# One decoder layer on one core: w_out split two units ahead, norms and token sums in pieces, first feed-forward matrix by column halves

## The chip, the cores and the metric

The kernel runs on one core of a Trainium2 chip. The metric is device time in microseconds (us) for the whole program, the median of several executions. Engines are named as in the profile: PE (matmuls), DVE and ACT (element work), POOL (element work on SBUF), SP (issues the loads and stores). L12 is line 12 of the kernel.

## What is computed

One layer of a hybrid decoder for 1024 tokens of width 1024, in float32. Every matmul is made of three: each operand is split into a high and a low part, and high*high, high*low and low*high are summed.

```python
h = rmsnorm(x, norm_mix_g)
u, q, kc, vc, ks, vs, kw, vw, g_nsa, g_br = split(h @ w_in)
y_a = s5_mixer(u, ...) @ w_up_ssm                  # state-space scan, GLU
kc, vc = gelu(blocks(kc) @ w1_k) @ w2_k, ...       # compress(): 63 blocks of 32 tokens
y_b = nsa_mixer(q, kc, vc, ks, vs, kw, vw, gates, rel_bias) @ w_up_nsa
g_a, g_b = split(sigmoid(g_br))
x = x + (g_a * y_a + g_b * y_b) @ w_out            # "merge"
h = rmsnorm(x, norm_ffn_g)
x = x + (silu(h @ w_ffn_gate) * (h @ w_ffn_up)) @ w_ffn_down
return rmsnorm(x, norm_final_g)
```

## The kernel before

There is no scheduler: each engine works through its instructions in the order in which the code issues them, and waits at the head of its queue. What waits there holds everything behind it.

**Input projection and S5.** `in_proj` is a generator whose steps are three matmuls of 128x512 each. `along(s5_params, 4.0)` and `along(s5, 3.0)` let that many projection steps follow each yield of the S5 code; afterwards `beside(proj, rest, 0.459)` lets 0.459 yields of `compress` and `glu` follow each projection step. The projection is thus the filling between dependent S5 and compress steps.

**compress.** `keys(0)` loads the tokens of the keys as `kk` (four DMAs of 252 KB), DVE adds positions into `kv` (L990), and PE multiplies with the `w1` pieces (L1004, 16 matmuls each). `kk` has one buffer, so `keys(1)` waits for the first add.

**Attention.** `up(a)` is a generator; its last parts store `pad` to DRAM (L1087) and its buffers are needed by the softmax transposes (`ready()`). `start(2)` issues the 12 loads of V.

**Weights.** `W.next(...)` hands out a unit of a weight matrix in high and low parts (`wh` by ACT, L396; `wl` by DVE, L399). It first splits up to the unit after the one handed out and loads up to four ahead. There are two raw buffers and three of `wh`/`wl`.

**Merge and first.** `merge` multiplies with `w_out` in 20 units of 256 rows and 512 columns (q is the half of the columns): two passes over token tiles (0,1,4,5), q=0 and q=1, one over (2,3,6,7) for q=0, then (2,3) and (6,7) apart for q=1. A tile's part of a unit is six matmuls (L1442 to L1444). After the last unit of a pass DVE adds x to each bank (`add`, L1448), and for q=1 ACT squares (L1452), takes the root (L413), and scales (`norm`, L1456). The normed tile is transposed by PE. For tiles 4 to 7 `turn` makes the token-side Winograd operands in five pieces, T1, B22, T3, T2 and T4, each split on ACT and DVE; their tiles are T1h/T1l (piece T3), T0h/T0l (piece T2) and T2h/T2l (piece T4). The feed-forward matrices are then multiplied by seven products each (`product(n, i)`, 12 matmuls; L227 to L229). `first` is the first matrix, n=0, during which tiles 6 and 7 are still being turned; `rest(n)` the others. On the weight side POOL scales by the norm's gain (`scale`, L171) and makes `sums` S (L204 to L207), and `t1` to `t4` split the parts for the products: (1,2), (6,5), (7,3), (4).

**down.** 44 units; `sr` is the hidden activation read back from DRAM. `after()` is run at three points inside the last `rest` and starts the loads and splits of down.

Of the kernel before, what the change touches and what calls it, by code (L numbers as in the profile page):

```python
# [8 lines left out]
F32 = mybir.dt.float32  # L9
# [7 lines left out]
P = 128  # L17
# [116 lines left out]
class Winograd:  # L134
# [87 lines left out]
    def product(self, n, i, ps, first=True):  # L222

        (wh, wl), (bh, bl) = self.w.pop((n, i)), self.B[i]
        mm = self.K.nc.tensor.matmul
        for k in range(4):
            mm(ps, wh[:, k], bh[:, k], start=first and k == 0, stop=False, skip_group_check=True)  # L227
            mm(ps, wh[:, k], bl[:, k], start=False, stop=False, skip_group_check=True)  # L228
            mm(ps, wl[:, k], bh[:, k], start=False, stop=k == 3, skip_group_check=True)  # L229
# [5 lines left out]
    def p1(self, n):  # L235
        K = self.K
        x = self.x[n] = K.bank("a")
        self.product(n, 1, x)
        p = self.p[n] = self.tile("p1")
        K.nc.scalar.copy(p, x)  # L240
# [11 lines left out]
    def p2(self, n):  # L252
        K, (name, j) = self.K, self.mats[n]
        x = self.x.pop(n)
        self.product(n, 2, x, first=False)
        t = self.tile("x11")
        if name == "w_ffn_gate":
            K.nc.scalar.activation(t, x, AF.Silu)
            self.gates[j, 0, 0] = t
        else:  # L260
            K.nc.vector.tensor_tensor(t, x, self.gates.pop((j, 0, 0)), op=OP.mult)
            K.nc.sync.dma_start(self.sd[2 * j][0], t)

    def first(self, turn):


        V, GP = self.K.nc.vector, self.K.nc.gpsimd
        self.p1(0)
        self.t2(0)
        self.p1(1)  # L270
        turn("transpose", 6)
        turn("T1", 6)
        self.p2(0)
        turn("transpose", 7)
        turn("T1", 7)
        self.t3(0)
        self.p2(1)
        z5, z3, v, y, c = (self.K.bank(t) for t in "aabbc")
        self.product(0, 5, z5)
        turn("B22", 6)  # L280
        turn("B22", 7)
        self.t4(0)
        self.load(2)
        self.product(0, 3, z3)
        turn("T3", 6)
        turn("T3", 7)
        self.product(0, 7, v)
        turn("T2", 6)
        turn("T2", 7)
        self.product(0, 6, y)  # L290
        turn("T4", 6)
        turn("T4", 7)
        u2, p5, u3 = self.p.pop(0), self.tile("p1"), self.tile("x11")
        self.K.nc.scalar.copy(p5, z5)
# [12 lines left out]

    def rest(self, n, early):

        K, last = self.K, n + 1 == len(self.mats)  # L310
        V, AC, GP = K.nc.vector, K.nc.scalar, K.nc.gpsimd
        y = K.bank("b")
        self.product(n, 6, y)
        u2 = self.p.pop(n)
        V.tensor_tensor(u2, u2, y, op=OP.add)
        if not early:
            self.p2(n)
            self.t4(n)
# [20 lines left out]
        if last:  # L339
            next(self.after)  # L340
# [19 lines left out]
class Kernel:  # L360
# [589 lines left out]
    def compress(self, pool):  # L950
# [9 lines left out]
        def keys(which):  # L960
            kk = pool.tile([P, 2, 1008], F32, name="kk", tag="kk", bufs=1)
            for g in range(2):
                src = self.cd[which, 64 * g:64 * g + 64, :]
                nc.sync.dma_start(kk[0:64, g, :], src[:, 0:1008])
                nc.sync.dma_start(kk[64:128, g, :], src[:, 16:1024])
            return kk

        kk = keys(0)
        src = [A["cmp_w1_" + kind].rearrange("(e l d) h -> e d l h", e=2, l=16) for kind in "kv"]

        def w1(j):
            w = pool.tile([P, 4, 256], F32, name="w1", tag="w1", bufs=4)
# [15 lines left out]
        for which in range(2):  # L988
            kv = pool.tile([P, 16, 126], F32, name="kv", tag="kv", bufs=2)
            V.tensor_tensor(kv, kk.rearrange("p g (n l) -> p l (g n)", l=16),  # L990
                            pt[:, which, :, None].to_broadcast([P, 16, 126]), op=OP.add)
            kvs.append(kv)
            if which == 0:
                kk = keys(1)
            yield
            yield
        hids = []
        for which in range(2):
            t = self.bank("c")
            for j in range(4):  # L1000
# [6 lines left out]
                if which == 0:  # L1007
                    ws.append(w1(j + 4))
# [160 lines left out]
    def attention(self, pools, loads, up):  # L1169
# [254 lines left out]
    def merge(self, pool, m, td, xd, ffn):  # L1424
# [21 lines left out]
        def add(tt, q, o):  # L1446
            x = x1[tt][:, 512 * q:512 * q + 512]
            V.tensor_tensor(x, x, o, op=OP.add)  # L1448
            if q:
                sq[tt] = pool.tile([P, 1], F32, name="ss", tag="ss", bufs=4)  # L1450
                xns[tt] = pool.tile([P, D], F32, name="xn", tag="xn", bufs=4)
                AC.activation(xns[tt], x1[tt], AF.Square, accum_out=sq[tt])  # L1452
                nc.sync.dma_start(xd[tt], x1[tt])

        def norm(tt):
            AC.activation(xns[tt], x1.pop(tt), AF.Copy, scale=self.rstd(pool, sq.pop(tt)))  # L1456

        def turn(what, tt):
# [3 lines left out]
            if what == "transpose":  # L1462
                xs, ps[tt] = xns.pop(tt), [self.bank(t) for t in "bc"]
# [5 lines left out]
            if what == "T1":  # L1469
# [6 lines left out]
                V.tensor_tensor(t3, b22, pb, op=OP.subtract)  # L1476
                x, o = t1, [x[:, 0:4, at] for x in m]
            else:
                b22, t1, t3 = tmp[tt]
            if what == "B22":  # L1480
# [12 lines left out]
        def turned(tt):  # L1493
            if tt < 4:
                self.transposed("bc", xns.pop(tt), m[0], m[1], tt)
            else:
                for what in ("transpose", "T1", "B22", "T3", "T2", "T4"):
                    turn(what, tt)

        def units(tts, q, between):  # L1500
            banks = [self.bank("a") for _ in tts]
            for u in range(4):
                w = unit(u, q)
                for f, *a in between.get((u, "w"), ()):
                    f(*a)
# [9 lines left out]
        units((0, 1, 4, 5), 0, {(0, "w"): [(load, tt) for tt in (0, 1, 4, 5)] + [(ffn.factors,)]})  # L1515
        units((0, 1, 4, 5), 1, {3: [(norm, 5)]})
        units((2, 3, 6, 7), 0, {0: [(turned, 0)], 1: [(turned, 1), (turned, 4)],
                                (1, "w"): [(load, 2), (load, 3)], (2, "w"): [(load, 6), (load, 7)],
                                2: [(turned, 5)], (3, "w"): [(ffn.load, 0)], 3: [(ffn.sums, 0)]})
        units((2, 3), 1, {3: [(norm, 3)]})  # L1520
        units((6, 7), 1, {1: [(turned, 2)], (2, "w"): [(ffn.load, 1)], 2: [(turned, 3), (ffn.t1, 0)],
                          (3, "w"): [(ffn.scale, 1), (ffn.t1, 1)], 3: [(norm, 7)]})
        ffn.first(turn)


# [20 lines left out]
    def down(self, pool, loads, xd):  # L1546

        nc, V, AC, mm = self.nc, self.nc.vector, self.nc.scalar, self.nc.tensor.matmul
        gf = self.broadcast_row(pool, "gfin", self.A["norm_final_g"])
# [19 lines left out]
        for n, (h, f) in enumerate(order):  # L1569
# [5 lines left out]
            wh, wl = self.W.next("w_ffn_down", P * f, 1, 0, D, ("act", "dve"))  # L1575
            if f == 16:
# [33 lines left out]
    def program(self):  # L1610
# [60 lines left out]
        beside(proj, side, 0.459)  # L1671
# [59 lines left out]
        def after():  # L1731
            loads[2](2)
# [3 lines left out]
            W.ahead(1, 2)  # L1736
            loads[3](1)
            yield
# [83 lines left out]
```

## Time and profile before

| | |
|---|---|
| runs | 1663.34, 1660.53, 1663.0 us; median 1663.0 |
| profiled execution | 1657.91 us, its span 1656.0 us |
| PE clock granted, mean | 0.974 of full speed |
| PE, DVE, ACT, POOL busy | 1568.5, 923.9, 628.2, 644.1 us |

Idle time of PE is what to look for, and stretches with the clock below 1. A time of a stretch is to be read against that stretch's own rows.

### The profile page before, as it was taken

To read this page: it belongs to the slowest core of one execution; us is meant where nothing else is said; L and a number is where in the kernel's file an instruction comes from. 1 tells how busy PE (TensorE), PEld (TensorE's weight loads), DVE (VectorE), ACT (ScalarE), POOL (GpSimd) and SP (SyncE) were. 2 spreads that over 40 slices of the span, in tenths; PEclk is the share of its full clock that TensorE was granted. 3 is DMA by queue.
4 is the path that set the end of the run, shared out by engine and by line. 5 is a ranking of instruction groups with operands and counts; after the bars stand their busy time and mean duration, and the time that the engine had idled before them with its cause. 6 is when DMAs were issued, how large, how long until landed. Compare 5 with 4: busy or idle time off the path is not lost.

```text
span 1656.0 us, 22273 instructions
## 1 busy us (share of the span) xinstructions
PE 1568.5 (95%) x7868; PEld 1312.0 (79%) x7868; DVE 923.9 (56%) x1738; ACT 628.2 (38%) x1272; POOL 644.1 (39%) x742
## 2 busy tenths in 40 slices
PE   8998999998998899998997889999999998999995
PEld 7776788887887799998886668888888886888884
DVE  7365787712335799998945565444444443334433
ACT  5221234312211698997014443233233332223422
POOL 1007767500121455554500328666776661000001
PEclk9999999999999999999998889999999999999998
DMA  7343343376338712102553422222322214454551
GB/s 216 103 131 98 100 137 92 92 166 160 120 114 226 202 34 60 42 27 61 194 165 128 153 70 77 89 84 82 95 78 89 77 52 159 152 184 157 181 188 60
DMA packets 164582, 194.27 MB, mean 117 GB/s; under 512 B 20730, under 2 KB 119446, under 8 KB 164471
## 3 DMA queue, kind: packets, MB, share of 16 engines
q1 hardware_dynamic: 164471, 192.85, 37.9%
q8 instruction: 63, 1.03, 0.3%
q14 instruction: 48, 0.39, 0.1%
HBM read 142.87 MB, written 47.84 MB: 115 GB/s over the span
## 4 chain that ended last, share of the span: by engine, by line
PE 75%; DVE 8%; DMA 6%; ACT 4%; issue 3%; POOL 1%; SPq 1%; POOLq 0%; DVEq 0%; ACTq 0%
PE a L387 6%; PE a L388 6%; PE a L389 6%; PE a L227 4%; PE a L228 4%; PE a L229 4%; PE O L1305 3%; PE S L1189 3%; PE T L1287 3%; PE a L1585 2%; PE a L1586 2%; PE a L1584 2%; PE b L229 2%; PE b L228 2%; PE b L227 2%
## 5 line engine op out<-in xcount | busy, mean ns | idle before, releaser
L399 DVE TENSOR_TENSOR wl<-wr,wh 128x1024 fp32r<-128x1024 f32 (+1 forms) x166 | 193.9, 1180 | 133.6 <-ACT wh L396 113.1
L387 PE MATMUL a<-hhi,wh 128*128 128x512 f32 x448 | 183.5, 410 | 0.0
L389 PE MATMUL a<-hhi,wl 128*128 128x512 f32 x448 | 178.6, 399 | 0.0
L388 PE MATMUL a<-hlo,wh 128*128 128x512 f32 x448 | 178.2, 398 | 0.0
L1260 POOL TENSOR_SCALAR P<-P,sum,gates 128x640 f32<-128x640 f32 (+3 forms) x192 | 124.7, 663 | 125.0 <-DVE sum L1254 65.5
L396 ACT CAST wh<-wr 128x1024 fp32r<-128x1024 f32 (+1 forms) x134 | 109.7, 837 | 163.6 <-DMA wr<-in_w_out 53.6
L228 PE MATMUL a<-mlo,wh 128*128 128x512 f32 x352 | 138.4, 393 | 1.9 <-DVE mlo L399 1.9
L227 PE MATMUL a<-mhi,wh 128*128 128x512 f32 x352 | 138.8, 394 | 0.5 <-ACT p L240 0.5
L229 PE MATMUL a<-mhi,wl 128*128 128x512 f32 x352 | 138.5, 394 | 0.0
L171 POOL TENSOR_SCALAR wr<-wr,gcol 128x256 f32<-128x256 f32 x176 | 92.6, 545 | 91.2 <-DMA wr<-in_w_ffn_gate 76.5
L394 POOL TENSOR_SCALAR wh<-wr 128x1024 fp32r<-128x1024 f32 x32 | 35.1, 1099 | 226.8 <-PE a L388 158.7
L1289 DVE TENSOR_TENSOR PTl<-T,PTh 128x512 fp32r<-128x512 f32 (+3 forms) x200 | 104.2, 544 | 15.5 <-ACT PTh L1288 14.0
L387 PEld LDWEIGHTS a<-hhi,wh 128*128 128x128 f32 x448 | 85.6, 191 | 23.9 <-issue 6.2
L389 PEld LDWEIGHTS a<-hhi,wl 128*128 128x128 f32 x448 | 85.3, 190 | 20.1
L399 DVE TENSOR_TENSOR slo<-sr,shi 128x512 fp32r<-128x512 f32 x44 | 31.5, 717 | 124.7 <-ACT shi L396 124.7
L388 PEld LDWEIGHTS a<-hlo,wh 128*128 128x128 f32 x448 | 85.6, 191 | 17.8
L1240 ACT ACTIVATE P<-P,m 128x640 f32<-128x640 f32 (+7 forms) x128 | 95.7, 747 | 9.5 <-DVE m L1224 9.5
L441 POOL TENSOR_SCALAR x1f<-x1f,rstd 128x1024 f32<-128x1024 f32 (+1 forms) x2 | 2.3, 1150 | 247.7 <-DVE rstd L421 242.7
L1288 ACT CAST PTh<-T 128x512 fp32r<-128x512 f32 (+3 forms) x200 | 88.5, 475 | 26.5 <-PE T L1287 19.4
L1287 PE MATMUL T<-cst,P 128*128 128x128 f32 x592 | 88.2, 276 | 8.3 <-DVE PTl L1289 7.8
L1224 DVE CUSTOM_DVE_ANT_0 P<-S,B 128x640 f32<-128x640 f32 (+7 forms) x128 | 89.5, 700 | 5.2 <-PE S L1189 3.0
L396 ACT CAST shi<-sr 128x512 fp32r<-128x512 f32 x44 | 27.3, 619 | 164.2 <-PE c L1585 149.0
(421 smaller groups left out, 4050.1 us busy)
## 6 DMA issues: line engine op xcount, KB each, us to landing
wr<-in_w_ffn_down SPq DMA_DIRECT2D x44, 512.0 KB, 3.4
wr<-in_w_in SPq DMA_DIRECT2D x28, 512.0 KB, 4.3
wr<-in_w_ffn_gate SPq DMA_DIRECT2D x22, 512.0 KB, 3.8
wr<-in_w_ffn_up SPq DMA_DIRECT2D x22, 512.0 KB, 4.1
sr<-sd SPq DMA_DIRECT2D x44, 256.0 KB, 3.6
wr<-in_w_out SPq DMA_DIRECT2D x20, 512.0 KB, 4.3
gd<-evf SPq DMA_DIRECT2D x32, 256.0 KB, 2.4
Q<-qd SPq DMA_DIRECT2D x64, 128.0 KB, 3.2
```

Source lines behind the costliest of these rows:

```text
L227: mm(ps, wh[:, k], bh[:, k], start=first and k == 0, stop=False, skip_group_check=True)
L228: mm(ps, wh[:, k], bl[:, k], start=False, stop=False, skip_group_check=True)
L229: mm(ps, wl[:, k], bh[:, k], start=False, stop=k == 3, skip_group_check=True)
L387: mm(ps, a, c, start=start and k == 0, stop=False, skip_group_check=True)
L388: mm(ps, a, d, start=False, stop=False, skip_group_check=True)
L389: mm(ps, b, c, start=False, stop=stop and k == nk - 1, skip_group_check=True)
L396: nc.scalar.copy(hi, src)
L399: (nc.gpsimd if lo_eng == "pool" else nc.vector).tensor_tensor(lo, src, hi, op=OP.subtract)
L1240: AC.activation(p[:, 0:nk], p[:, 0:nk], AF.Exp, bias=m[:, 0:1], scale=-1.0, accum_out=sm(0))
L1260: sc = lambda x, y, z: GP.tensor_scalar(x, x, a[:, y:y + 1], gate(z), op0=OP.mult, op1=OP.mult)
L1287: T.transpose(t[:, x, :], p[:, c:c + P], self.ident)
L1289: V.tensor_tensor(ol, t[:, 0:len(cc), :], oh, op=OP.subtract)
```

## The change

It reorders; it computes the same, with 60 more PE instructions (five products are made in two halves of 256 columns).

1. The paces 4.0, 3.0 and 0.459 become 4.6, 3.2 and 0.6.
2. compress loads both `kk` up front (two buffers), ahead of `w1` (three buffers instead of four).
3. The remaining parts of `up(a)` run at the start of `start(2)`, ahead of the V loads.
4. In merge the split of unit u+2 is issued after the first tile of unit u (`W.ahead(2, 4)`). `square`, `root` and `norm` are separate and placed by hand; the pieces of `turn` for tiles 4 and 5 are spread over the units. In `first` both p1 products come up front, norms of tiles 6 and 7 are interleaved, and products 5, 6, 3, 7 and 4 are made by column halves: half 0 (tiles 4, 5) early, half 1 (tiles 6, 7) late.
5. down: four `sr` loads early, `gfin` later, and the third step of `after()` ahead of a store.

```diff
-    def first(self, turn):
+    def first(self, norms, turn):
...
-        self.p1(0)
+        x0, x1 = self.x[0], self.x[1] = bank("a"), bank("a")
+        self.product(0, 1, x0)
+        self.product(1, 1, x1)
+        next(norms)
         self.t2(0)
-        self.p1(1)
-        turn("transpose", 6)
+        next(norms)
+        self.p1out(0)
+        z5 = bank("a")
+        self.product(0, 5, z5, half=0)
+        turn("transpose", 6, "bc")
+        next(norms)
+        self.p1out(1)
+        turn("sums", 6)
+        y = bank("b")
+        self.product(0, 6, y, half=0)
...
+        self.product(0, 6, y, half=1)
+        self.sums(1)
+        AC.copy(p5, z5)
+        self.t2(1)
         V.tensor_tensor(u2, u2, y, op=OP.add)
         V.tensor_tensor(u3, u2, v, op=OP.add)
         V.tensor_tensor(u2, u2, z3, op=OP.add)
-        self.sums(1)
-        self.t2(1)
-        self.product(0, 4, c)
         GP.tensor_tensor(u2, u2, p5, op=OP.add)
         GP.tensor_tensor(p5, u3, p5, op=OP.add)
+        self.product(0, 4, c, half=1)
...
+        if last:
+            next(self.after)
         self.out(n, 1, 1, p5)
...
-            kk = pool.tile([P, 2, 1008], F32, name="kk", tag="kk", bufs=1)
+            kk = pool.tile([P, 2, 1008], F32, name="kk", tag="kk", bufs=2)
...
-        kk = keys(0)
+        ks = [keys(0), keys(1)]
...
-        ws = [w1(j) for j in range(4)]
+        ws = [w1(j) for j in range(3)]
...
             if n == 2:
+                run(up)
                 load_v(0, 5, 3)
...
                 for i, tt in enumerate(tts):
                     part(w, u, tt, banks[i])
+                    if i == 0:
+                        self.W.ahead(2, 4)
+                        for f, *a in between.get((u, "m"), ()):
+                            f(*a)
                     if u == 3:
                         add(tt, q, banks[i])
-                        if q and i:
-                            norm(tts[i - 1])
+                        if q and tt < 6:
+                            square(tt)
+                            if i:
+                                root(tts[i - 1])
...
-        units((0, 1, 4, 5), 1, {3: [(norm, 5)]})
-        units((2, 3, 6, 7), 0, {0: [(turned, 0)], 1: [(turned, 1), (turned, 4)],
+        units((0, 1, 4, 5), 1, {3: [(norm, 0)]})
+        units((2, 3, 6, 7), 0, {(0, "m"): [(norm, 1), (root, 5), (norm, 4), (norm, 5)], 0: [(turned, 0)],
...
+                                (3, "m"): [(ffn.load, 0)] + T(5, "transpose", "sums", "T1")})
+        units((2, 3), 1, {0: T(5, "B22", "T3"), 1: T(5, "T2"), 2: T(5, "T4") + [(ffn.sums, 0)]})
...
-            loads[2](2)
+            loads[2](4)
...
-            W.ahead(1, 2)
             loads[3](1)
+            W.ahead(1, 3)
...
-        along(self.s5_params(), 4.0)
+        along(self.s5_params(), 4.6)
...
-        along(self.s5(), 3.0)
+        along(self.s5(), 3.2)
...
-        beside(proj, side, 0.459)
+        beside(proj, side, 0.6)
```

How the order moves at three places. ACT at the first four norms (tiles 0, 1, 4, 5) stood like this before; the first row is the root of tile 0, and `xn<-x_..,rstd` is a norm:

```order
L413 ACTIVATE rstd<-ss,eps 128x1
L1456 ACTIVATE xn<-x_8713,rstd 128x1024
L1452 ACTIVATE xn,ss<-x_8717 128x1024
L413 ACTIVATE rstd<-ss,eps 128x1
L1456 ACTIVATE xn<-x_8715,rstd 128x1024
L1452 ACTIVATE xn,ss<-x_8719 128x1024
L413 ACTIVATE rstd<-ss,eps 128x1
L1456 ACTIVATE xn<-x_8717,rstd 128x1024
L413 ACTIVATE rstd<-ss,eps 128x1
L1456 ACTIVATE xn<-x_8719,rstd 128x1024
L396 CAST wh<-wr 128x1024
```

and now, in the same engine and place:

```order
L438 ACTIVATE rstd<-ss,eps 128x1
L1479 ACTIVATE xn,ss<-x_8729 128x1024
L438 ACTIVATE rstd<-ss,eps 128x1
L1479 ACTIVATE xn,ss<-x_8731 128x1024
L438 ACTIVATE rstd<-ss,eps 128x1
L1486 ACTIVATE xn<-x_8725,rstd 128x1024
L421 CAST wh<-wr 128x1024
L1486 ACTIVATE xn<-x_8727,rstd 128x1024
L438 ACTIVATE rstd<-ss,eps 128x1
L1486 ACTIVATE xn<-x_8729,rstd 128x1024
L1486 ACTIVATE xn<-x_8731,rstd 128x1024
```

The next pass's `wh`, which stood behind four norms, now stands behind one, and it is the unit after the next. DVE at the end of the pass over tiles 2, 3, 6, 7 had the turning of tile 5 whole, then a split, then the four adds:

```order
L1488 TENSOR_TENSOR t_9185<-mhi,t_9184 128x512
L1489 TENSOR_TENSOR t_9185<-t_9185,mlo 128x512
L399 TENSOR_TENSOR T2l<-t_9185,T2h 128x4x128
L399 TENSOR_TENSOR wl<-wr,wh 128x1024
L1448 TENSOR_TENSOR x_9067<-x_9067,a 128x512
L1448 TENSOR_TENSOR x_9069<-x_9069,a 128x512
L1448 TENSOR_TENSOR x_9145<-x_9145,a 128x512
L1448 TENSOR_TENSOR x_9147<-x_9147,a 128x512
```

and now the adds stand behind the first pieces of tile 5's turning, the rest of them after the adds:

```order
L424 TENSOR_TENSOR wl<-wr,wh 128x1024
L1516 TENSOR_TENSOR t_9206<-b,mhi 128x512
L1517 TENSOR_TENSOR t_9206<-t_9206,mlo 128x512
L1518 TENSOR_TENSOR t_9207<-b_9205,b 128x512
L424 TENSOR_TENSOR mlo<-t_9206,mhi 128x4x128
L1472 TENSOR_TENSOR x_9079<-x_9079,a 128x512
L1472 TENSOR_TENSOR x_9081<-x_9081,a 128x512
L1472 TENSOR_TENSOR x_9146<-x_9146,a 128x512
L1472 TENSOR_TENSOR x_9148<-x_9148,a 128x512
L424 TENSOR_TENSOR wl<-wr,wh 128x1024
L424 TENSOR_TENSOR mlo<-b_9205,mhi 128x4x128
```

The transposes that feed these pieces are issued in the middle of the pass's last unit. At the end of `first` DVE had (L295 to L297 the three adds that POOL waits for, `wl<-S` the split t2(1)):

```order
L399 TENSOR_TENSOR T2l<-t_9571,T2h 128x4x128
L295 TENSOR_TENSOR p_9505<-p_9505,b 128x512
L296 TENSOR_TENSOR x_9681<-p_9505,b 128x512
L297 TENSOR_TENSOR p_9505<-p_9505,a 128x512
L399 TENSOR_TENSOR wl<-S,wh 128x1024
```

and now:

```order
L424 TENSOR_TENSOR T2l<-t_9599,T2h 128x4x128
L424 TENSOR_TENSOR wl<-S,wh 128x1024
L322 TENSOR_TENSOR p_9521<-p_9521,b 128x512
L323 TENSOR_TENSOR x_9729<-p_9521,b 128x512
L324 TENSOR_TENSOR p_9521<-p_9521,a 128x512
```

The split has moved ahead of the three adds.

## Rows read from the trace of the kernel before

**Rows 1.** The page's first part, PE: busy us (share of the span), instructions.

```profile
PE 1568.5 (95%) x7868; PEld 1312.0 (79%) x7868; DVE 923.9 (56%) x1738; ACT 628.2 (38%) x1272; POOL 644.1 (39%) x742
```

**Rows 2.** Windows, PE: length and PE busy in us, PEclk, DMA share, GB/s.

```profile
380.00:400.00 20.00, 17.74 (x99) 0.84 0.52 119
520.00:560.00 40.00, 28.28 (x141) 0.91 0.87 252
827.00:903.00 76.00, 67.27 (x299) 0.95 0.41 139
903.00:960.00 57.00, 44.64 (x171) 0.83 0.47 157
960.00:988.20 28.20, 23.87 (x91) 0.88 0.21 66
1400.00:1420.00 20.00, 19.54 (x71) 0.83 0.52 182
```

**Rows 3.** Timeline of PE, first matmuls after waits: start, us, [idle before <-releaser].

```profile
140.30 0.97 PE L891 MATMUL b<-cst,w 128*128 128x128 f32 x4 [2.82 <-DVE w L854]
...
178.74 1.47 PE L910 MATMUL b<-ut,wt 128*128 128x128 f32 x11 [2.42 <-DVE wt L892]
...
381.08 3.75 PE L1004 MATMUL c<-kv,w 128*128 128x126 f32 x16 [4.97 <-DVE kv L990]
388.82 2.02 PE L1004 MATMUL c<-kv,w 128*128 128x126 f32 x16 [1.18 <-DMA w<-in_cmp_w_v]
...
553.45 1.90 PE L1287 MATMUL T<-cst,P 128*128 128x128 f32 x8 [5.12 <-DVE PTl L1289]
...
882.51 0.80 PE L1442 MATMUL a<-wh,mhi 128*128 128x512 f32 x1 [4.04 <-ACT wh L396]
...
914.53 0.47 PE L1442 MATMUL a<-wh,mhi 128*128 128x512 f32 x1 [3.03 <-DVE x L1448]
...
995.21 0.50 PE L229 MATMUL b<-T1h,wl 128*128 128x512 f32 x1 [0.53 <-DVE wl L399]
...
1400.00 0.80 PE L1584 MATMUL a<-wh,shi 128*128 128x512 f32 x1 [4.82 <-ACT wh L396]
```

**Rows 4.** Timeline of PE where product(1,6) starts.

```profile
988.25 0.39 PE L227 MATMUL b<-T0h,wh 128*128 128x512 f32 x1
988.48 0.39 PE L228 MATMUL b<-T0l,wh 128*128 128x512 f32 x1
```

**Rows 5.** Timelines of SP in compress, and of SP and ACT at attention's start.

```profile
351.94 0.53 SPq L964 DMA_DIRECT2D kk<-cd  x1
...
546.98 0.82 SPq L1087 DMA_DIRECT2D pad<-sga  x2
...
552.00 1.07 ACT L1288 CAST PTh<-T 128x512 fp32r<-128x512 f32 x2 [6.23 <-issue]
```

**Rows 6.** Timelines of ACT and DVE in merge and first: `wh`, a token split, `wl`.

```profile
881.43 1.03 ACT L396 CAST wh<-wr 128x1024 fp32r<-128x1024 f32 x1
...
979.47 0.69 DVE L399 TENSOR_TENSOR T0l<-t,T0h 128x512 fp32r<-128x512 f32 x1 [0.69 <-ACT T0h L396]
...
987.53 1.22 DVE L399 TENSOR_TENSOR wl<-S,wh 128x1024 fp32r<-128x1024 f32 x1
```

**Rows 7.** Timelines of DVE and POOL while POOL makes sums.

```profile
969.08 3.15 DVE L399 TENSOR_TENSOR mlo<-b,mhi 128x512 fp32r<-128x512 f32 x2
...
970.09 1.59 POOL L205 TENSOR_TENSOR S<-S,wr 128x512 f32<-128x512 f32 x1
```

**Rows 8.** Timelines of POOL and ACT behind the three adds, start of rest(1).

```profile
987.76 2.14 POOL L301 TENSOR_TENSOR p<-p,p 128x512 f32<-128x512 f32 x1 [12.70 <-DVE p L297]
989.97 1.28 POOL L302 TENSOR_TENSOR p<-x,p 128x512 f32<-128x512 f32 x1
...
991.29 1.15 ACT L246 ACTIVATE p<-p 128x512 f32<-128x512 f32 x2 [5.01 <-POOL p L302]
```

**Rows 9.** The page's sixth part: w_out loads, KB each, us to landing.

```profile
wr<-in_w_out SPq DMA_DIRECT2D x20, 512.0 KB, 4.3
```

More of the change, by code (lines that the diff above doesn't have):

```diff
@@ L220, in t4, with product @@
             self.r.pop(n)
-    def product(self, n, i, ps, first=True):
-        (wh, wl), (bh, bl) = self.w.pop((n, i)), self.B[i]
-        mm = self.K.nc.tensor.matmul
+    def product(self, n, i, ps, first=True, half=None):
+        (wh, wl), (bh, bl) = self.w[n, i], self.B[i]
+        c = slice(0, 512) if half is None else slice(256 * half, 256 * half + 256)
+        if half != 0:
+            self.w.pop((n, i))
+        mm, o = self.K.nc.tensor.matmul, ps[:, c]
         for k in range(4):
-            mm(ps, wh[:, k], bh[:, k], start=first and k == 0, stop=False, skip_group_check=True)
-            mm(ps, wh[:, k], bl[:, k], start=False, stop=False, skip_group_check=True)
-            mm(ps, wl[:, k], bh[:, k], start=False, stop=k == 3, skip_group_check=True)
+            mm(o, wh[:, k], bh[:, k, c], start=first and k == 0, stop=False, skip_group_check=True)
+            mm(o, wh[:, k], bl[:, k, c], start=False, stop=False, skip_group_check=True)
+            mm(o, wl[:, k], bh[:, k, c], start=False, stop=k == 3, skip_group_check=True)
     def tile(self, name, bufs=3):
@@ L235, in p1, with p1out @@
     def p1(self, n):
-        K = self.K
-        x = self.x[n] = K.bank("a")
+        x = self.x[n] = self.K.bank("a")
         self.product(n, 1, x)
+        self.p1out(n)
+    def p1out(self, n):
         p = self.p[n] = self.tile("p1")
-        K.nc.scalar.copy(p, x)
+        self.K.nc.scalar.copy(p, self.x[n])
     def out(self, n, i, h, t):
@@ L252, in p2, with p2out @@
     def p2(self, n):
-        K, (name, j) = self.K, self.mats[n]
-        x = self.x.pop(n)
-        self.product(n, 2, x, first=False)
+        self.product(n, 2, self.x[n], first=False)
+        self.p2out(n)
+    def p2out(self, n):
+        K, (name, j), x = self.K, self.mats[n], self.x.pop(n)
         t = self.tile("x11")
@@ L338, in rest @@
         self.t2(n + 1)
-        if last:
-            next(self.after)
         c = K.bank("c")
@@ L1449, in add, with square, root, norms @@
             if q:
-                sq[tt] = pool.tile([P, 1], F32, name="ss", tag="ss", bufs=4)
-                xns[tt] = pool.tile([P, D], F32, name="xn", tag="xn", bufs=4)
-                AC.activation(xns[tt], x1[tt], AF.Square, accum_out=sq[tt])
                 nc.sync.dma_start(xd[tt], x1[tt])
-        def norm(tt):
-            AC.activation(xns[tt], x1.pop(tt), AF.Copy, scale=self.rstd(pool, sq.pop(tt)))
-        def turn(what, tt):
+        def square(tt):
+            ss = pool.tile([P, 1], F32, name="ss", tag="ss", bufs=4)
+            xns[tt] = pool.tile([P, D], F32, name="xn", tag="xn", bufs=4)
+            AC.activation(xns[tt], x1[tt], AF.Square, accum_out=ss)
+            sq[tt] = ss
+        def root(tt):
+            sq[tt] = self.rstd(pool, sq[tt])
+        def norm(tt):
+            AC.activation(xns[tt], x1.pop(tt), AF.Copy, scale=sq.pop(tt))
+        def norms():
+            square(6)
+            root(6)
+            yield
+            norm(6)
+            square(7)
+            root(7)
+            yield
+            norm(7)
+            yield
+        def turn(what, tt, tags="bc"):
             at, c = slice(P * tt, P * tt + P), slice(P * (tt - 4), P * (tt - 4) + P)
@@ L1462, in turn @@
             if what == "transpose":
-                xs, ps[tt] = xns.pop(tt), [self.bank(t) for t in "bc"]
+                xs, ps[tt] = xns.pop(tt), [self.bank(t) for t in tags]
                 for h in range(2):
@@ L1468, in turn @@
                 return
-            if what == "T1":
+            if what == "sums":
                 pb, pc = (p.rearrange("p (k t) -> p k t", k=4) for p in ps.pop(tt))
@@ L1476, in turn @@
                 V.tensor_tensor(t3, b22, pb, op=OP.subtract)
+                return
+            b22, t1, t3 = tmp[tt]
+            if what == "T1":
                 x, o = t1, [x[:, 0:4, at] for x in m]
-            else:
-                b22, t1, t3 = tmp[tt]
-            if what == "B22":
+            elif what == "B22":
                 x, o = b22, [x[:, 4:8, at] for x in m]
@@ L1493, in turned @@
         def turned(tt):
[L1494 to L1498, printed above, removed]
+            self.transposed("bc", xns.pop(tt), m[0], m[1], tt)
         def units(tts, q, between):
@@ L1520, in merge @@
[L1520 to L1523, printed above, removed]
+        T = lambda tt, *what: [(turn, w, tt) for w in what]
+        units((0, 1, 4, 5), 0, {(0, "m"): [(load, tt) for tt in (0, 1, 4, 5)] + [(ffn.factors,)]})
+        units((0, 1, 4, 5), 1, {3: [(norm, 0)]})
+        units((2, 3, 6, 7), 0, {(0, "m"): [(norm, 1), (root, 5), (norm, 4), (norm, 5)], 0: [(turned, 0)],
+                                (1, "m"): [(load, 2), (load, 3)],
+                                1: [(turned, 1)] + T(4, "transpose", "sums", "T1"),
+                                (2, "m"): [(load, 6), (load, 7)], 2: T(4, "B22", "T3", "T2", "T4"),
+                                (3, "m"): [(ffn.load, 0)] + T(5, "transpose", "sums", "T1")})
@@ L1526, in down_loads @@
+        units((2, 3), 1, {0: T(5, "B22", "T3"), 1: T(5, "T2"), 2: T(5, "T4") + [(ffn.sums, 0)]})
+        units((6, 7), 1, {(0, "m"): [(norm, 2), (root, 3)], 0: [(norm, 3)], 1: [(turned, 2), (ffn.load, 1)],
+                          2: [(turned, 3), (ffn.t1, 0), (ffn.scale, 1)], (3, "m"): [(ffn.t1, 1)]})
+        ffn.first(norms(), turn)
     def down_loads(self, pool, sd):
@@ L1575, in down @@
             wh, wl = self.W.next("w_ffn_down", P * f, 1, 0, D, ("act", "dve"))
+            if n == 16:
+                gf = self.broadcast_row(pool, "gfin", self.A["norm_final_g"])
             if f == 16:
```

44 lines of the change are left out of this document (20 added, 24 removed).

## The prediction

> **What bounds the kernel now.** I read the page's first part, the windows of PE, its waits and its timeline, in this order. PE is busy for 95% of the span [rows 1], so only what PE loses can be won: its idle time, and the stretches in which the clock falls to its lower level, 1.2 GHz, after such idle time. In a window with granted clock c and length T the clock costs about (1-c)*T, because at 1.2 GHz a matmul of 128x512 takes twice its usual 0.227 us (988.25 to 988.48 [rows 4]). The windows show where the loss lies: 827 to 988, merge and the first feed-forward matrix; smaller ones in compress, at the start of attention, and at the start of down [rows 2].
>
> Merge and first, up to the start of product(1,6) at 988.25 [rows 4]: PE idles 76.0-67.3 plus 57.0-44.6 plus 28.2-23.9, 25.4 us; the clock costs 0.05*76 + 0.17*57 + 0.12*28.2, 16.9 us [rows 2]. With the wait of 0.53 in product(1,7) [rows 3] 42.8 us are lost, and that is all that reordering can give back there. The pattern of the losses is a norm or a turning ahead of something that PE needs: the next pass's `wh` behind four norms (4.04), the banks behind DVE's adds (3.03) [rows 3].
>
> **The change part by part**, against the profiled execution's own 1657.9 us.
>
> *Paces.* More projection steps of 0.69 us (three matmuls) fall beside the S5 parameters, where PE waits for DVE's chain (2.82 and 2.42 [rows 3]) and the clock falls after it. By the order of PE, 11 more steps are done by the end of the parameters, but only those that stand behind a waiting matmul's predecessors fill its wait. I take -4; bounds 0 (the chains start later by as much) and -9 (all such waits of that stretch and their clock gone).
>
> *compress.* The wait for the second `kv` (4.97) and one for `w1` (1.18) [rows 3] go with both `kk` up front, and with them a clock loss of 0.16*20, 3.2 us [rows 2]: 9.4 in all. But the first `w1` now lands behind 2.0 MB of `kk` instead of 1.0, and with pace 0.6 fewer projection steps (20 in the order of PE, 26 before; 14 us against 18) cover the loads. At 210 to 250 GB/s, an estimate from the 252 GB/s of the densest window [rows 2], 2.0 MB and the first 0.5 MB take 10 to 12 us from the first `kk` issue (351.94 [rows 5]), and some 2 to land: PE arrives 5 to 7 us too early, and its clock falls once more. Late next is thus the first `w1` instead of the second `kv`. I take 0; bounds -5 and +4.
>
> *Attention's start.* The last two `pad` stores are issued at 546.98 behind V's loads, and the first `PTh` waits until 552.00 for them [rows 5]; PE waits 5.12 [rows 3]. With the stores ahead of V's loads this wait goes, but the V loads start later and the scores of step 2 stand behind three more parts of `up`. Late next are V's loads, for the first values. I take -3; bounds 0 and -6 (the wait and a clock loss after it).
>
> *Merge and first.* I walked through the new order of the queues with the durations of before: `wh` 1.03, `wl` 1.22, a token split 0.69 [rows 6]. Gone is the `wh` wait at each change of pass, since the split is made two units ahead and one norm, not four, stands before it. What is left, each at its place:
> - the four banks of the (2,3,6,7) pass are freed behind three pieces and one split of tile 5's turning, which wait for transposes issued in the middle of the last unit: 3.7;
> - first norm to transposes, bank and one late `wl`: 2.7;
> - norm of tile 2 to its transposes: 2.5;
> - t2(0), behind the chain of tile 6's norm, for the first half of product 5: 3.3;
> - tile 7's T2 piece for the late half of product 6, 2.2, and its T4 piece for that of product 4, 4.1: these five-piece chains are as long as before, and only the work in front of them has moved.
>
> Together 18.5. Then something new: at the end of `first` the split t2(1) (1.22 [rows 6]) has gone ahead of the three adds for which POOL waits. POOL's two adds take 3.4 us, and behind them ACT stands with the output's three scalings before t3(1), which product(1,7) needs [rows 8]. Counted from the T4 piece of tile 7, product(1,7) can start at 11.7 us and PE is there at 8.5: 3.1, and 0.7 for its `wl`. In all 22.3 of idle time, and 1 for the 60 additional matmuls. For the clock I take 3: of the waits left only three are over 3 us, against seven before, which took 16.9. So 42.8 - 26.3: -17. The unknowns: the clock, 0 to 14, and the waits, 10 to 26; bounds -30 and -2.
>
> POOL's sums beside DVE are the place where a duration is not fixed: two token splits took 3.15 us there instead of 1.38 [rows 6, 7], and the sums stand beside the T1 and B22 pieces of tiles 6 and 7, as before. The Trainium skill says in "SBUF — State Buffer", "Who interferes with whom", that a VectorE instruction with two SBUF inputs contends with a GpSimd instruction that reads SBUF, and in "SBUF: two separate sides" that the one that comes second is blocked for the whole instruction. The trace agrees (1.6 us each beside a POOL operation of 1.59). By it nothing is won by spreading the pieces while POOL works: each waits out one sum. I take that as a rival.
>
> *down.* The wait for the third `wh` (4.82 [rows 3]) and the clock after it (0.17*20, 3.4 [rows 2]) are 8.2 us. `sr` and the weights of the third unit now come in time. But the first raw weight lands behind four `sr`, and DVE's last add of `rest`, which frees a bank that down's first unit needs, stands behind two of down's splits. I estimate 3 of new wait and 2 of clock: -3; bounds -8 and +1. `gfin` later costs nothing: POOL is idle there, and the norm that needs it comes 20 units later.
>
> The sum: -4 + 0 - 3 - 17 - 3 = -27, so 1631 on the scale of the profiled execution. The median of the runs is 1663.0, 5 us above that execution, and the lowest run 2.6 above it; I put the forecast at **1635** on the scale of the median.
>
> **The rivals.**
> - *All waits of merge close.* The chains overlap with the products' early halves better than my walk has it, and only 6 us are left with no clock loss: merge -36, down and paces at their bounds, together about -53: 1610. For it speaks that the early halves give PE 7 us of work that needs no late tile; against it that T2 and T4 of tile 7 still end the chain.
> - *DVE is held up by POOL.* If the sums fall beside the T2 and T4 pieces, which nothing covers, eight splits and subtractions wait out a sum each: four operations of 1.6 against 0.69, some 4 to 7 us on the path, and after a longer wait the low clock once more, 5 to 8: merge -4 to -6, together about -15: 1648. By the rule of the Trainium skill above this is what happens whenever the two meet.
> - *It loses.* The splits two ahead stand at the heads of ACT and DVE and wait for the load of their raw weights, of which there are but two buffers. A load takes 4.3 us [rows 9], cast and split 2.3 [rows 6], so two buffers give a unit each 3.3 us at best, where a unit of two tiles takes PE 2.7. If squares and adds stand behind such a split for more than 1.4 us in each of the 20 units, 28 us, it eats the sum: at 2 us 40 are lost, 1676. Against it: the DMA engines are busy for only 0.41 and 0.47 of these windows [rows 2], and the first 12 units take 5.4 us of PE each.
> - *It changes nothing.* The waits move to where the next chain ends, as in compress: merge -2, the others 0 or given back: 1660.
>
> **How the numbers follow.** The forecast's case, -15 to -40, 0.62 (1622 to 1648); all closed, 0.12 (1600 to 1622); DVE held up, 0.17 (1643 to 1657); nothing, 0.04; a loss, 0.05. The range of 8 in 10 leaves out half of the closed case and what lies above DVE's: 1616 to 1653. A measurement tells 0.2% (3.3 us) from no change; by the cases, 0.91 faster, 0.04 the same, 0.05 slower.
>
> **What would show it.** Right: PE's waits for `wh` at the changes of pass are gone; a wait of 3 to 4 us at the pass (2,3) for banks, one of 3 at product(1,7), waits for T0l and T2l in the late halves; the time from the first w_out matmul to the start of product(1,6) is 139 to 146 us, not 161; the `kv` wait in compress is replaced by one at the first L1004; no PE wait of 5 us before the first PTh. Wrong: ACT or DVE idle on DMA ahead of a w_out split with squares or adds behind it; DVE rows of 1.5 to 3 us for T0l and T2l beside POOL; the clock still 0.83 in the second half of merge; a first L1004 that waits 10 us or more.

## The result and the profile after

The changed kernel takes 1635.02 us (median of 4 runs, 1632.34 to 1639.17), before 1662.99: ratio 0.9837, 95% interval 0.9814 to 0.986. Its profiled execution took 1635.29 us with a span of 1633.4, that of before 1657.91 and 1656.0; so the two profiles differ by 22.6 us where the medians differ by 28.0. The profile of before was a quick one, that of after an ordinary one, and what follows from the traces is measured against 22.6.

Four points of PE's timeline part the program: the first score matmul of attention, the first w_out matmul of merge, the first one of down, and the end. Before they stand at 526.79, 827.09, 1383.86 and 1656.0; after:

```profile
526.41 1.76 PE L1212 MATMUL S<-KS,Q 128*128 128x512 f32 x6 [2.90 <-DVE sga L1108]
...
821.70 0.40 PE L1466 MATMUL a<-wh,mhi 128*128 128x512 f32 x1
...
1365.61 0.40 PE L1632 MATMUL a<-wh,shi 128*128 128x512 f32 x1
```

The gain is thus 0.4 us up to attention, 5.0 in attention, 12.9 from merge to down, 4.4 in down. The windows of PE after (length, busy, granted clock, DMA share, GB/s) answer to [rows 2]:

```profile
130.00:200.00 70.00, 64.68 (x321) 0.98 0.33 98
345.00:405.00 60.00, 54.48 (x304) 0.94 0.70 169
405.00:520.00 115.00, 111.44 (x478) 0.99 0.49 146
520.00:560.00 40.00, 34.25 (x193) 0.96 0.76 236
...
822.00:903.00 81.00, 75.45 (x334) 0.96 0.55 182
903.00:930.00 27.00, 24.20 (x106) 0.94 0.44 138
930.00:945.00 15.00, 12.62 (x64) 0.89 0.31 105
945.00:960.00 15.00, 12.70 (x94) 1.00 0.27 81
960.00:968.00 8.00, 5.47 (x22) 0.55 0.05 16
968.00:980.00 12.00, 11.48 (x44) 0.87 0.07 17
```

and before the first three of them were

```profile
130.00:200.00 70.00, 61.88 (x312) 0.95 0.26 79
345.00:405.00 60.00, 53.84 (x293) 0.94 0.78 180
405.00:520.00 115.00, 115.00 (x501) 1.00 0.49 147
```

From 130 to 200 us PE idles 2.8 us less, and the clock's cost, (1-c)*T, falls by 2.1: the paces' gain of 4.9. From 405 to 520 PE idles 3.6 more, at a clock that costs 1.2 more: 4.7 back. The waits of PE that matter, from its timeline (start, us, [idle before <-releaser]), to be held against [rows 3]:

```profile
144.22 0.50 PE L412 MATMUL a<-hhi,wh 128*128 128x512 f32 x1 [0.72 <-POOL wh L419]
146.33 0.50 PE L414 MATMUL a<-hhi,wl 128*128 128x512 f32 x1 [1.37 <-DVE wl L424]
158.66 1.60 PE L935 MATMUL b<-ut,wt 128*128 128x128 f32 x6 [2.50 <-issue]
379.05 1.19 PE L1027 MATMUL c<-kv,w 128*128 128x126 f32 x4 [5.52 <-DMA w<-in_cmp_w_k]
472.71 0.79 PE L414 MATMUL a<-hhi,wl 128*128 128x512 f32 x1 [2.59 <-DVE wl L424]
...
897.11 0.76 PE L1466 MATMUL a<-wh,mhi 128*128 128x512 f32 x1 [3.85 <-ACT mhi L421]
915.06 0.49 PE L1466 MATMUL a<-wh,mhi 128*128 128x512 f32 x1 [1.43 <-ACT wh L421]
...
935.85 0.39 PE L230 MATMUL a<-mhi,wh 128*128 128x256 f32 x1 [1.63 <-ACT wh L421]
959.99 0.38 PE L230 MATMUL b<-T0h,wh 128*128 128x256 f32 x1 [1.56 <-ACT T0h L421]
965.40 0.58 PE L230 MATMUL c<-T2h,wh 128*128 128x256 f32 x1 [2.03 <-ACT T2h L421]
976.83 0.50 PE L232 MATMUL b<-T1h,wl 128*128 128x512 f32 x1 [0.52 <-DVE wl L424]
1370.18 0.62 PE L1632 MATMUL a<-wh,shi 128*128 128x512 f32 x1 [1.88 <-DVE p L363]
```

The wh waits at the changes of pass and the 5 us before the first PTh are gone; the second kv's wait is replaced by one for the first w1. The wait at the start of the pass (2,3) is 3.85 where 3.7 was forecast for its banks. That it is for a bank is read from DVE's four adds, of which the first, of 0.68 us, frees a bank and ends 0.15 before PE starts; the profile names ACT there:

```profile
896.28 2.48 DVE L1472 TENSOR_TENSOR x<-x,a 128x512 f32<-128x512 f32 x4
```

From the first w_out matmul to the third of product(1,7) it takes 155.1 us (before 168.1). To the start of product(1,6) it takes 147.1 us, so this sign, 139 to 146, was missed.

There is one wait for wh that the walk did not have: 1.43 us at 915.06, with 0.76 for wl behind it, one unit after the change to the pass (6,7). The last pieces of tile 5's turning now stand beside POOL's first sums (905.93 to 912.86), and the wh that PE waits for stands behind them on ACT:

```profile
906.27 1.51 DVE L424 TENSOR_TENSOR T0l<-t,T0h 128x512 fp32r<-128x512 f32 x1 [0.69 <-ACT T0h L421]
907.71 2.31 DVE L424 TENSOR_TENSOR wl<-wr,wh 128x1024 fp32r<-128x1024 f32 x1
909.94 1.77 DVE L1531 TENSOR_TENSOR t<-mhi,t 128x512 f32<-128x512 f32 x1
911.75 1.67 DVE L1532 TENSOR_TENSOR t<-t,mlo 128x512 f32<-128x512 f32 x1
```

```profile
907.31 1.62 POOL L205 TENSOR_TENSOR S<-S,wr 128x512 f32<-128x512 f32 x1
```

```profile
913.45 0.62 ACT L421 CAST T2h<-t 128x512 fp32r<-128x512 f32 x1 [6.25 <-DVE t L1532]
913.97 1.04 ACT L421 CAST wh<-wr 128x1024 fp32r<-128x1024 f32 x1
```

Before, POOL's first sums came only at 923.82, and the same split of tile 5 took 0.69:

```profile
908.91 0.69 DVE L399 TENSOR_TENSOR T0l<-t,T0h 128x512 fp32r<-128x512 f32 x1 [0.69 <-ACT T0h L396]
```

### The profile page after: what moved, and what is told of

Its sections match the earlier page's. It is cut to its first block, busy times and chain, and to the rows that moved or that the text cites. A ratio compares the mean times of both kernels' runs of the same rounds, so it can differ in the third digit from the quotient of the medians.

```text
span 1633.4 us, 22403 instructions
## 1 busy us (share of the span) xinstructions
PE 1565.5 (96%) x7928; PEld 1313.2 (80%) x7928; DVE 925.3 (57%) x1738; ACT 627.9 (38%) x1271; POOL 643.6 (39%) x742
## 4 chain that ended last, share of the span: by engine, by line
PE 83%; DVE 6%; DMA 4%; ACT 3%; issue 2%; SPq 1%; POOL 1%; POOLq 0%; DVEq 0%; ACTq 0%
PE a L412 7%; PE a L414 7%; PE a L413 7%; PE a L232 5%; PE a L230 5%; PE a L231 5%; PE O L1328 4%; PE T L1310 4%; PE S L1212 3%; PE a L1632 2%; PE a L1633 2%; PE a L1634 2%; PE b L230 2%; PE b L232 2%; PE b L231 2%
## 5 line engine op out<-in xcount | busy, mean ns | idle before, releaser
L230 PE MATMUL a<-mhi,wh 128*128 128x512 f32 (+1 forms) x360 | 139.2, 387 | 1.6 <-ACT wh L421 1.6
L232 PE MATMUL a<-mhi,wl 128*128 128x512 f32 (+1 forms) x360 | 139.1, 386 | 0.8 <-DVE wl L424 0.8
L231 PE MATMUL a<-mlo,wh 128*128 128x512 f32 (+1 forms) x360 | 138.8, 385 | 0.0
L424 DVE TENSOR_TENSOR wl<-S,wh 128x1024 fp32r<-128x1024 f32 x44 | 65.6, 1490 | 42.4 <-ACT wh L421 39.7
```

Of the source, the lines that this page charges most:

```text
L230: mm(o, wh[:, k], bh[:, k, c], start=first and k == 0, stop=False, skip_group_check=True)
L231: mm(o, wh[:, k], bl[:, k, c], start=False, stop=False, skip_group_check=True)
L232: mm(o, wl[:, k], bh[:, k, c], start=False, stop=k == 3, skip_group_check=True)
L424: (nc.gpsimd if lo_eng == "pool" else nc.vector).tensor_tensor(lo, src, hi, op=OP.subtract)
```

## The experiments

Medians; each ratio is to the kernel before, run on the same chip.

| run | us | 95% interval of the ratio |
|---|---|---|
| paces_back | 1633.05 | 0.9809 to 0.9839 |
| pace3_back | 1627.59 | 0.9780 to 0.9809 |
| w1_first | 1640.32 | 0.9852 to 0.9881 |
| merge_back | 1648.06 | 0.9893 to 0.9926 |
| one_ahead | 1634.99 | 0.9815 to 0.9882 |
| whole_products | 1630.85 | 0.9796 to 0.9841 |
| up_back | 1638.03 | 0.9834 to 0.9878 |
| down_back | 1637.70 | 0.9833 to 0.9879 |
| late_halves | 1635.78 | 0.9835 to 0.9864 |
| turn_first | 1638.66 | 0.9845 to 0.9880 |
| adds_first | 1633.73 | 0.9823 to 0.9852 |
| combined | 1627.03 | 0.9787 to 0.9815 |

A difference of 3 us between two of them is no more than executions of one program differ: the first score matmul, before which one_ahead, whole_products, late_halves, turn_first and adds_first have the same code, stands between 526.9 and 530.2. So the parts of merge are compared by points of the timeline, counted from the first w_out matmul.

These points scatter too. Six executions have merge and first as in the changed kernel: that kernel's own and those of paces_back, pace3_back, w1_first, up_back and down_back. In them product(1,6) starts at 145.6 to 149.3, and the third matmul of product(1,7) comes at 153.7 to 157.3. They part mostly in the 8 us from 115 on, where the granted clock is 1.00 in down_back, 0.79 in the changed kernel and 0.57 to 0.62 in the others. The changed kernel, down_back and paces_back there:

```profile
936.70:944.70 8.00, 7.59 (x42) 0.79 0.26 77
```

```profile
937.61:945.61 8.00, 7.58 (x52) 1.00 0.25 77
```

```profile
933.03:941.03 8.00, 7.29 (x35) 0.58 0.29 88
```

One profile thus does not show a difference of a few us in merge; what lies outside the six is said below. The scatter in attention (295.1 to 296.2 us, up_back left out) and in down (265.7 to 268.8, down_back left out) is smaller.

**paces_back.**

```diff
-        along(self.s5_params(), 4.6)
+        along(self.s5_params(), 4.0)
-        along(self.s5(), 3.2)
+        along(self.s5(), 3.0)
-        beside(proj, side, 0.6)
+        beside(proj, side, 0.459)
```

> The changed kernel with the three old paces (4.0, 3.0, 0.459), all else as changed. Theory A: the new paces win 4 to 5 us of waits and clock beside the S5 parameters (130 to 200 us) and give as much back where the projection ends (405 to 520 us), since the projection's last weight splits then stand on DVE behind the GLU; so the total stays within 2 us, 1633 to 1638, with the waits back at 140 to 180 and gone at 455 and 472. Rival B: the paces win 4 and it is the loads of compress that take it back; then this kernel is 4 to 5 us slower than the changed one, about 1640.

1633.05: no slower with the old paces, within theory A's bound. Beside the S5 parameters the waits are back (first row below), and PE no longer waits for weights at the projection's end: attention starts at 522.01, 4.4 earlier than with the new paces. In compress the waits for w1 are 3.18 and 1.83. Rival B falls.

**pace3_back.** Only the third of these lines goes back.

> The changed kernel with only the third pace back at 0.459 (the other two stay 4.6 and 3.2). Theory A: the waits of the projection's last steps at 455 and 472 go and the first L1027 waits less than 3 us (26 projection steps cover the loads, not 20): 5 to 8 us faster, 1627 to 1630. Rival B: the steps done early are missing at the end whatever the third pace is: the wait for weights moves, and the time stays within 2 us of 1635.

1627.59 us, 7.4 less than the changed kernel, and attention starts at 518.85. The windows of PE in pace3_back, after one of paces_back, show both sides:

```profile
130.00:200.00 70.00, 61.69 (x315) 0.95 0.27 80
```

```profile
130.00:200.00 70.00, 64.67 (x324) 0.98 0.32 98
200.00:345.00 145.00, 145.00 (x780) 1.00 0.38 102
345.00:405.00 60.00, 57.15 (x325) 1.00 0.79 186
```

The two S5 paces keep their gain, and compress, with 26 projection steps as cover, now wins as well: the first L1027 waits 1.74 instead of 5.52, a later one 1.12, and the clock stays up. The third pace was the part of the change that lost. By the windows most of what comes back lies in compress, 345 to 405 us: 2.7 of idle time and 3.6 of clock. Of the waits at the projection's end one remains (1.59 at 442.25), 2.0 less in all, and the clock no longer falls there (1.2); the wait for the gates at attention's start is longer, 5.62 for 2.90, and takes 2.7 back.

**w1_first.**

```diff
-        ks = [keys(0), keys(1)]
+        ks = [keys(0)]
...
-        ws = [w1(j) for j in range(3)]
+        ws = [w1(0), w1(1)]
+        ks.append(keys(1))
+        ws.append(w1(2))
```

> The changed kernel with the first two w1 pieces loaded ahead of the second kk, the third behind it. Theory A (the first w1 lands late because 2.0 MB of kk stand before it): the wait of 5.5 us at the first L1027 falls below 1.5 and 3 to 6 us are won, 1629 to 1632. Rival B (the sum of bytes binds, the second kk is then late for its kv): the wait moves to the fifth group of 16 matmuls, within 2 us of 1635.

1640.32, slower, which neither expected; attention starts at 532.06, later than in any run with the same code but for these loads (526.4 to 530.2). The first wait falls to 1.43, as theory A has it; but two others follow, 2.36 at 383.44 and the one in the first row, on PE, DVE and SP of w1_first:

```profile
393.30 3.75 PE L1029 MATMUL c<-kv,w 128*128 128x126 f32 x16 [4.82 <-DMA w<-in_cmp_w_k]
```

```profile
382.01 3.55 DVE L1017 TENSOR_TENSOR kv<-kk,pt 128x2016 f32<-128x2016 f32 x1 [7.27 <-DMA kk<-cd]
385.47 2.35 DVE L424 TENSOR_TENSOR wl<-wr,wh 128x1024 fp32r<-128x1024 f32 x2
...
386.72 0.38 SPq L94 DMA_DIRECT2D wr<-in_w_in  x1
387.20 1.26 SPq L999 DMA_DIRECT2D w<-in_cmp_w_k  x2
```

The second kk lands later and DVE stands at its add until 382.0, with two splits of projection weights behind it (385.47). The next projection load, which stands ahead of the fourth w1 on SP, is issued at 386.72 and that w1 at 387.20 (382.83 in the changed kernel). That the load waited for the raw buffer which those splits free is read from their order and times, not tested.

**merge_back.** `merge` and `first` of the kernel before, with all else as changed.

> The changed kernel with merge and first as they were before (splits one unit ahead, norms and turning whole, no column halves); paces, compress, attention and down as changed. Theory A (merge gives 13 to 14 us by the markers of the two profiles): 1648 to 1650. Rival C (merge was worth the 17 of the forecast, and profiles of before and after differ by luck): 1652 or more. Rival D (other parts carry more): 1645 or less.

1648.06, as theory A has it: merge and first are worth 13.0 by the medians, and from the first w_out matmul to down's first it takes 558.5 us instead of 543.9 (the six executions: 542.4 to 546.0).

**one_ahead.**

```diff
                     if i == 0:
-                        self.W.ahead(2, 4)
                         for f, *a in between.get((u, "m"), ()):
```

> The changed kernel without the line that splits two units of w_out ahead in the middle of a unit; the separate norms, the spread turning and the column halves stay. Theory A (the split ahead is what keeps wh in time behind the norms): waits for wh come back at the changes of pass, two or three of 2 to 4 us with their clock, 4 to 10 us slower, 1639 to 1645. Rival B (parting the norms is enough, and the split ahead only moves work): within 2 us of 1635.

1634.99: rival B. Product(1,6) starts 146.7 us after the first w_out matmul, with the line 147.1; no wait for wh above 1.4 us comes back. The split two ahead, first in the change's title, shows no worth here. What won must be in the rest of merge and first; the parted norms and the spread turning were not undone by themselves.

**whole_products.** The five calls with `half=0` are taken out, and those with `half=1` made whole.

> The changed kernel with the five products of the first matrix whole, each where its late half stands; all else as changed. Theory A (the early halves give PE 7 us of work while the chains of tiles 6 and 7 run on ACT and DVE, and cost 1 us of issue): 4 to 8 us slower, 1639 to 1643, with longer waits for the T pieces before the products. Rival B (the end of the T4 chain of tile 7 sets product(1,6), and the early halves only shift idle time): within 2 us.

1630.85: no slower, so the halves win nothing and theory A falls. By the timeline the third matmul of product(1,7) comes at 152.4, earlier than in any of the six (153.7 to 157.3), while product(1,6) starts at 145.9, among them. That the halves lose something is likely, but this one execution does not say how much; combined, also with whole products, has 154.8.

**late_halves.** Both halves of each product one behind the other, at the late place.

> The changed kernel with the five products still in two halves of 256 columns, but both halves one behind the other at the late place, so that only the early place is undone. Theory A (the early half of product 5 and the split t2(0) stand on PE and ACT ahead of tile 6's transposes and so delay the chain of T pieces that sets the end): like whole products, 1631 to 1632, tile 6 transposed some 2 us earlier than in the changed kernel. Rival B (the halves lose by their 256 columns, 60 more matmuls and the low clock they run at): 1634 to 1636, no better than the changed kernel.

1635.78, but its attention starts 3.7 late, in code that was not changed. By the timeline product(1,7) comes at 153.4, between whole_products and the earliest of the six. What the early place costs and what the columns cost is not told apart.

**turn_first.**

```diff
         next(norms)
-        self.t2(0)
         next(norms)
+        self.t2(0)
         self.p1out(0)
         z5 = bank("a")
-        self.product(0, 5, z5, half=0)
         turn("transpose", 6, "bc")
+        self.product(0, 5, z5, half=0)
```

> The changed kernel with halves kept early, but tile 6's norm ahead of the split t2(0) on ACT and its transposes ahead of the first half of product 5 on PE. Theory A (the chain of T pieces sets the end, and whatever stands before its head costs): 3 to 5 us faster than the changed kernel, 1630 to 1632, with the waits for T0h and T2h in the late halves 1 us or less. Rival B (PE then idles at the head of first for t2(0) as long as it gains at the end): within 2 us of 1635.

1638.66, product(1,7) at 157.7: no gain, so theory A falls; that it is slower is not shown, as the six reach 157.3. Tile 6 is transposed 3.0 earlier than in the changed kernel, but the last of the T pieces comes 2.6 later. What these pieces wait for is seen in combined, below.

**adds_first.** The three adds of `first` ahead of `self.t2(1)`.

> The changed kernel with the three adds of the first matrix ahead of the split t2(1) on DVE, as before. The forecast's step (the split ahead of the adds makes product(1,7) wait 3.8 us): 2 to 4 us faster. Theory A (PE reaches product(1,7) 2.3 us late since product(1,6) runs at the low clock, and POOL's adds took 2.6 and not 3.4; there is 0.5 us of wait to win, and the split for product(1,6) comes 2 us later): within 1 us of 1635, with a wait for wl at product(1,6) in place of the one at product(1,7).

1633.73, product(1,7) at 154.3, among the six. Its wait is gone, as it is in three of the six without this edit, and none for wl comes at product(1,6). The forecast's 3.8 is not there: the most that the six wait at product(1,7) is 0.99 and 0.53, in up_back.

**up_back.** Without `run(up)` in `start(2)`.

> The changed kernel without running the rest of up(a) ahead of the V loads. Theory A (the pad stores behind the V loads hold the first PTh): the wait of 5 us at the second group of softmax transposes is back, 4 to 6 us slower, 1639 to 1641. Rival B (the late V loads take back half of it): 2 to 3 us slower.

1638.03; from the first score to the first w_out matmul it takes 299.5 us instead of 295.3, and the wait is back, as in [rows 3]:

```profile
553.58 1.94 PE L1310 MATMUL T<-cst,P 128*128 128x128 f32 x8 [5.17 <-DVE PTl L1312]
```

**down_back.** `loads[2](2)`, the old order of `after()` and its third step, gfin first.

> The changed kernel with the start of down as it was (two sr loads early, old order of splits and of the third step, gfin first). Theory A (the wait for the third wh, 4.8 us, and its clock return, against a bank wait of 1.9 now): 3 to 5 us slower, 1638 to 1640, with the wait back at down's third unit. Rival B (it depends on when the hidden activation is stored, not on the loads' order): within 2 us.

1637.70, and from down's first matmul to the end it takes 272.2 us instead of 267.8. The wait of 4.61 for wh at the third unit is back; theory A.

**combined.** pace3_back, whole_products and adds_first together, and

```diff
-        self.product(0, 2, x0, first=False)
         turn("transpose", 7, "ac")
+        self.product(0, 2, x0, first=False)
```

> What the runs before point to, together: the changed kernel with the third pace back at 0.459, the five products of the first matrix whole at their late places, the three adds ahead of the split t2(1), and tile 7's transposes ahead of the product (0,2). By theory A (from tile 7's transposes to its T4 piece DVE and ACT take 20.5 us whatever PE does, so product(1,6) moves with those transposes): 7.5 us from the pace, 2.7 from the whole products, up to 2 from the transposes, 0.8 from the adds: 1622 to 1625, the transposes at 118.4 us after the first w_out matmul and the T4 piece's low part 20.5 behind them. Rival B (DVE is bound by its own queue there, not by the transposes): the T4 piece comes 141 us after the first w_out matmul, as with whole products, 1625 to 1627.

1627.03: 2.0% below the kernel before, and no better than pace3_back alone. Tile 7's transposes come at 118.1 as expected, 2.4 earlier than in whole_products, yet the T4 piece comes at 143.9, not at 138.6: theory A falls in its form, and 141 of rival B is missed too. DVE and ACT of combined show what the chain waits for:

```profile
935.94 1.05 ACT L416 CAST wh<-S 128x1024 fp32r<-128x1024 f32 x1 [3.89 <-PE a L231]
...
937.02 1.23 DVE L419 TENSOR_TENSOR wl<-S,wh 128x1024 fp32r<-128x1024 f32 x1 [4.17 <-ACT wh L416]
...
956.36 0.69 DVE L419 TENSOR_TENSOR T2l<-t,T2h 128x512 fp32r<-128x512 f32 x1 [0.68 <-ACT T2h L416]
```

The split t3(0) waits for a PE matmul of L231 into bank a, that is, for product(0,2): there are three wh buffers, and t3(0) takes the one that product(0,2) reads last. All of tile 7's pieces stand behind that split on ACT and DVE. From its wl to tile 7's T2l it is 19.3 to 19.4 us in the changed kernel, whole_products, late_halves, turn_first, adds_first and combined alike (whole_products: 943.59 and 962.97), and in the other executions of the changed merge, while the distance from tile 7's transposes is 20.4 to 20.5 in the first five and 25.7 in combined. So the end of product(0,2) sets product(1,6): the early halves of products 5 and 6 stand in front of it on PE, and so do tile 7's transposes in combined. There product(0,2) starts 2.7 later than in whole_products, since PE waits 1.23 for tile 7's norm and the clock from 115 to 123 is 0.59 instead of 0.79. Where the six executions part, they part by the same rule: with a lower clock product(0,2) ends later, and the T pieces move with it. All this is read from the traces; a fourth wh buffer, or t3(0) behind the turning of tile 7, was not tried.

## Why the prediction was right, and where not

The forecast of 1635 is met at the median. On the scale of the profiles it said -27 and -22.6 was measured; the two agree at the median because before's profile was 5 us below its own median, which is luck and no merit of the sum. The errors of the terms also offset one another in part. By its terms:

- *Paces, -4.* Right in place and size (4.9 between 130 and 200 us), but the term stopped there: up to attention only 0.4 was won. I priced the third pace only by the cover that compress loses. At 0.6 the GLU runs beside the projection's last steps, and the split of their weights stands on DVE behind the GLU's product, which waits for ACT: 4.7 us at 405 to 520. With this pace back 3.1 of them go; the larger part of what it cost, 6.3, was in compress after all, where the forecast had looked.
- *compress, 0.* Right: the waits for the second kv and for w1 with their clock (9.4) went, and 5.5 with its clock came at the first w1. The third pace made it nothing: with 0.459 the same loads leave 1.74 and 1.12 (with the old S5 paces too, 3.18 and 1.83).
- *Attention, -3.* The mechanism is right, the size 5.0 (4.2 by up_back): no wait of PE is for V's late loads.
- *Merge and first, -17.* 12.9 measured, 13.0 to 14.6 by merge_back; the six executions are 10.8 to 14.4 below the kernel before and 12.5 to 16.1 below merge_back, so the term was too large by more than the scatter. The waits left are where the walk put them (3.85 for 3.7; 1.63 and 0.75 for 3.3; 1.9 and 2.0 for 2.2 and 4.1), but for the 1.43 and 0.76 at 915, and come to 16.1 rather than 22.3. The step that failed is the clock, 3 in the sum: from 822 to 980 us (1-c)*T comes to 11.7. Of this 5.0 lies at 959 to 971 us, where PE has little work between the waits of the two late halves and runs at 1.2 GHz for most of the time, and nearly all the rest at 896 to 945, behind the waits of 3.85, 1.43 and 1.63. The new wait of 3.8 at product(1,7) measured 0.52: POOL's two adds took 2.6 instead of 3.4, and PE came 2.3 us later than I had it, at the low clock. And I credited the split two ahead, beside the parted norms, with the end of the wh waits; one_ahead shows that those of 3 us and more stay away without it.
- *down, -3.* 4.4; the new bank wait is 1.88 where 3 was put.

None of the rivals happened whole, but a part of one did. For tiles 6 and 7 POOL's sums slowed T1 and B22 pieces, as before (two mlo splits 2.37), and T0l and T2l took 0.69. For tile 5 the change moved the T2 and T4 pieces beside POOL's first sums: a T0l of 1.51, two subtractions of 1.77 and 1.67 and a wl of 2.31, together 4.0 us more than alone. That is the rival *DVE is held up by POOL* and the sign given for it, DVE rows of 1.5 to 3 us, which the forecast looked for only in tiles 6 and 7. PE's waits of 1.43 and 0.76 stand behind it, and after them the clock, 0.66 in the 5 us from 915 on, costs an estimated 1.7; no run shows what goes without it.

## What to carry to other kernels

A filler that runs out early is paid for at its end: price a pace over the whole stretch in which the filler is used, and by the queue on which the filler's own weights are split. Where engines work in order, look for the oldest instruction that the last chain stands behind, with what frees its buffer; work that looks free because it fills an early wait may stand in front of just that. Of a change in many parts, undo each: here one part, the third pace, cost 7 us of what the rest had won, and the first named showed no worth. And before small differences of a stretch are read from single profiles, compare the same stretch in runs whose edits lie elsewhere: here the same code of merge and first differed by up to 3.6 us.

## What the runs showed of the hardware

PE's clock fell after waits that were short. In the changed kernel PE idled 1.56 and 2.03 us before the late halves of products 6 and 4, and the window from 960 to 968 was granted 0.55, nearly all of it 1.2 GHz; after the waits of 1.43 and 0.76 at 915 the next 5 us were granted 0.66. In whole_products, with one wait of 1.90 there, the window from 960 to 968 has 0.79. Before, most of the falls in merge had come with waits of 3 us and more [rows 3]; of two waits of 1.9 in first one was followed by a fall (0.67 from 972 to 976 us), the other by none (1.00 from 985 to 989). At the low level matmuls of 128x512 follow one another at 0.43 us (897.67 to 898.10 in the changed kernel), 1.9 times 0.227 and not quite the twice of the prediction.

DVE's operations on SBUF took longer beside POOL's sums: 1.51 to 1.77 us for 128x512 and 2.31 for 128x1024 in the rows above, against 0.69 and 1.23 alone.
